# Norms between the stages of a two-block network: order of issue, two engines for the squares, one step less in the mean square

## The chip, the core and the metric

One core of a Trainium2 chip. The metric is device time in microseconds, from the runs of the whole program. The core has TensorE (PE, matmuls and transposes; PEld is its weight load), VectorE (DVE), ScalarE (ACT) and GpSimd (POOL), each with a queue of its own that it works off in order; DMAs are issued from SyncE's queue (SP) and a few from POOL's.

## What is computed

Two blocks on 512 tokens of width 1024, in fp32: a first block with two layers (a token mixer of mLSTM, Fourier and convolution branches, then an MLP with squared ReLU), where layer 0 also works on 256 context tokens, and a second block with two layers of retention, sparse attention and gated linear attention. Around each mixer and MLP stands the same frame:

```python
def rmsnorm(x, g):
    y = xf * lax.rsqrt(jnp.mean(xf * xf, axis=-1, keepdims=True) + EPS)
    return (y * g).astype(x.dtype)

hx = modulate(rmsnorm(x, g_pre_mix[l]), mx[0], mx[1])      # pre-norm, gain and shift
...
x = x + mx[2] * rmsnorm(out_x, g_post_mix[l])              # post-norm and update
hx = modulate(rmsnorm(x, g_pre_mlp[l]), mx[3], mx[4])      # pre-norm of the next stage
x = x + mx[5] * rmsnorm(sq_relu_mlp(hx, w_mlp1[l], w_mlp2[l]), g_post_mlp[l])
```

The post-norm and update of one stage and the pre-norm of the next follow each other directly. This is the work between the stages.

## The kernel before

Tokens are worked on in tiles of 128 rows (four of x, two of the context), and a tile of 128x1024 is kept as two halves of 512 columns. Every fp32 matmul is made of three (mm3, L316 to L318), from a high and a low part of each operand. The weights come by DMA in chunks of 128x1024 (tile `st`), ACT casts the chunk to its high part (`whi`, L283) and DVE subtracts to get the low part (`wlo`, L284). There are three buffers for `st` and four each for `whi` and `wlo` (wload).

The stage ends are project (an output projection, L588 and square_sum) and the last block of mlp (L667, L670). For each token tile i they leave two halves of output times the post gain, and the sum of squares. Then `leave` puts a function `norm` on the list `normed`. When it is called, it does this for the tile:

- update (L503): inv_rms turns the two sums into 1/rms by three POOL steps (L453 add, L454 scale and add EPS, L346 power of -0.5). DVE then makes x = x + o * r for each half, and x goes to DRAM.
- for tile 0, the gains of the next stage (gain_of, L1169), and the steps of the modulation (ada_task, whose products are L381 on POOL with a sum on ACT, and L384 on DVE) that are still missing for them.
- prenorm_a: two squares with row sums on ACT (L465), inv_rms, then the scaling of one half on ACT (L467) and the other on DVE (L468).

It then puts prenorm_b on the list `turned`: per half, four transposes on PE into a PSUM tile `s` (L351; three buffers), gain and shift by turns on ACT (L482) and DVE (L485), and the split into the high part (ACT L312) and the low part (DVE L312) that the next stage's matmuls read.

`flush(n, m)` works off both lists down to n and m entries. `leave` calls it with 1 and 1, so a tile's norm is traced one tile later and its turn two tiles later; `ready`, called at each matmul group of the next stage, works off what that group needs. In flush, `issue_after` queues the ACT instructions of a norm behind the latest square_sum and the PE instructions of a turn behind the latest matmul.

What sets the order: a planner lays out every engine's queue before the run. Of the instructions that it takes to be ready it places the one traced earliest; those traced in a `high_priority` block come before all others, and among themselves in the order of tracing. The weight chunks (DMA, cast, subtraction), project's square_sum and post gain, and the evacuations of PSUM are traced so. The norms and turns of flush are not, except the context's at the very start.

Stretches named A to E in this text are the five stage ends that feed a next stage: A the projection of layer 0 (context and x), B the MLP of layer 0 (both), C the projection and D the MLP of layer 1 (x), E the first projection of the second block. The last projection writes the result.

Of the kernel before, what the change touches and what calls it, by code (L numbers as in the profile page):

```python
# [13 lines left out]
AF = mybir.ActivationFunctionType  # L14
OP = mybir.AluOpType

P = 128
D = 1024
# [3 lines left out]
EPS = 1e-6  # L22
# [203 lines left out]
class Net:  # L226
# [140 lines left out]
    def ada_task(self, w, j, vecs, mods, bias, post=None, key=None):  # L367


        nc = self.nc  # L370
        part = self.small("adp", [P, 2, 8, 2])
        for f in range(8):
            st = self.hp.tile([P, D], F32, tag="sa", name=self.nm("sa"), bufs=NSA)
            nc.sync.dma_start(st, w[f])
            for m, v in enumerate(vecs):
                row = self.cond_row(v)
                for h in range(2):
                    e = slice(512 * h, 512 * h + 512)
                    x, o = self.slot(), part[:, m, f, h:h + 1]
                    if m:  # L380
                        nc.gpsimd.tensor_mul(x, st[:, e], row[:, e])  # L381
                        nc.scalar.activation(x, x, AF.Copy, accum_out=o)
                    else:
                        nc.vector.tensor_tensor_reduce(x, st[:, e], row[:, e], 1.0, 0.0, op0=OP.mult, op1=OP.add,  # L384
                                                       accum_out=o)
            yield
        for m, mod in enumerate(mods):
            e = slice(8 * j, 8 * j + 8)
            nc.vector.tensor_add(mod[:, e], part[:, m, :, 0], part[:, m, :, 1])
            nc.vector.tensor_add(mod[:, e], mod[:, e], bias[:, e])  # L390
            if post is not None:
                g = self.small("gv", [P, 8])
                nc.vector.tensor_mul(g, mod[:, e], post)
                ps = self.psum("s")
                self.transpose(ps[:8, :P], g)
                row = self.small("gvt", [8, P])
                nc.vector.tensor_copy(row, ps[:8, :P])
                d = self.grows[key + (m,)] = self.dp.tile([8, P], F32, tag="gr%d%d%d%d" % (*key, m), name=self.nm("gr"))
                nc.sync.dma_start(d, row)
# [50 lines left out]
    def inv_rms(self, ss):  # L450

        v = self.small("ms", [P, 1])
        self.nc.gpsimd.tensor_add(v, ss[:, 0:1], ss[:, 1:2])  # L453
        self.nc.gpsimd.tensor_scalar(v, v, 1.0 / D, EPS, op0=OP.mult, op1=OP.add)  # L454
        return self.rsqrt(v, 1)

    def square_sum(self, src, acc):
# [2 lines left out]
    def prenorm_a(self, xh):  # L460
        nc = self.nc
        xn = [self.slot(), self.slot()]
        ss = self.small("ss", [P, 2])
        for j in range(2):
            nc.scalar.activation(xn[j], xh[j], AF.Square, accum_out=ss[:, j:j + 1])  # L465
        r = self.inv_rms(ss)
        nc.scalar.activation(xn[0], xh[0], AF.Copy, scale=r)  # L467
        nc.vector.tensor_scalar_mul(xn[1], xh[1], r)  # L468
        return xn
# [78 lines left out]
    def flush(self, n, m):  # L548

        while len(self.normed) > n:  # L550
            with self.tc.issue_after(self.last_sq):
                self.normed.pop(0)[2]()
        while len(self.turned) > m:
            with self.tc.issue_after(self.last_mm):
                self.turned.pop(0)[2]()

    def ready(self, h, i, ahead):
# [609 lines left out]
    def gain_of(self, tag, mod, j, base):  # L1167
        g = self.small(tag, [P, 8])
        self.nc.vector.scalar_tensor_tensor(g, mod[:, 8 * j:8 * j + 8], 1.0, base, op0=OP.add, op1=OP.mult)  # L1169
        return g  # L1170

    def first_block(self):
# [717 lines left out]
```

## Time and profile before

| | before |
|---|---|
| median of 3 runs | 2880.83 us (2879.89 to 2881.83) |
| the profiled execution | 2877.77 us, span of its instructions 2875.7 us |
| mean granted TensorE clock | 0.973 |
| PE busy | 2686.8 us, 93% |
| DVE, ACT, POOL busy | 60%, 40%, 16% |
| DMA | 312.85 MB, 109 GB/s |

The span runs from the first to the last instruction; times in the rows are counted from its start. An engine's busy share is over the whole span, in which stages with different limits follow each other.

### The profile page before, as it was taken

What the parts mean: (1) busy time and instruction counts of PE and PEld (TensorE: products, weight loads), DVE (VectorE), ACT (ScalarE), POOL (GpSimd) and SP (SyncE); (2) the same over time, 40 slices, a digit from 0 to 9 for tenths busy, and PEclk for the clock granted to TensorE, in tenths of its full rate; (3) what the DMA queues carried; (4) which work ended last, traced back from release to release, by engine and by line L of the source; (5) the groups of instructions that cost most, each with busy time, mean ns of one, the idle gap of its engine ahead of it and who ended that gap; (6) DMA issues with size and microseconds to landing.
All of it is one profiled execution on the core that took longest, in us unless ns stands there. A gap on an engine that the chain in (4) does not pass through costs nothing. (4 is left out here: it accounts for less than half of the span.)

```text
span 2875.7 us, 36809 instructions
## 1 busy us (share of the span) xinstructions
PE 2686.8 (93%) x13684; PEld 2161.2 (75%) x13684; DVE 1737.3 (60%) x3619; ACT 1158.1 (40%) x2224; POOL 455.0 (16%) x548
## 2 busy tenths in 40 slices
PE   6877998999999998998999989999999999999998
PEld 2766787888888876787878867776788777767887
DVE  3799756466555578955566457666433567664334
ACT  2644545444222264545323353435222543353222
POOL 2365302233000013201000010010012100101011
PEclk9989999999999999999999999999999999999999
DMA  8322224334433443224464332211132412111223
GB/s 272 115 78 83 90 70 147 125 119 131 139 119 132 131 141 111 88 88 147 159 200 157 115 121 87 83 60 52 37 103 95 147 67 96 52 59 37 96 88 117
DMA packets 101283, 312.85 MB, mean 109 GB/s; under 512 B 11504, under 2 KB 15368, under 8 KB 101104
## 3 DMA queue, kind: packets, MB, share of 16 engines
q1 hardware_dynamic: 100544, 309.64, 32.5%
q8 instruction: 107, 1.75, 0.3%
q0 software_dynamic: 560, 0.86, 0.1%
q14 instruction: 72, 0.59, 0.1%
HBM read 293.43 MB, written 17.03 MB: 108 GB/s over the span
## 5 line engine op out<-in xcount | busy, mean ns | idle before, releaser
L316 PE MATMUL mm<-xhi,whi 128*128 128x512 f32 (+2 forms) x1520 | 598.3, 394 | 41.9 <-DVE sl L779 29.1
L284 DVE TENSOR_TENSOR wlo<-st,whi 128x1024 fp32r<-128x1024 f32 x352 | 448.7, 1280 | 281.9 <-ACT whi L283 276.1
L283 ACT CAST whi<-st 128x1024 fp32r<-128x1024 f32 x352 | 369.9, 1052 | 565.8 <-PE mm L317 284.7
L317 PE MATMUL mm<-xlo,whi 128*128 128x512 f32 (+2 forms) x1520 | 593.3, 390 | 0.4 <-DVE xlo L312 0.2
L318 PE MATMUL mm<-xhi,wlo 128*128 128x512 f32 (+2 forms) x1520 | 592.6, 390 | 0.0
L316 PEld LDWEIGHTS mm<-xhi,whi 128*128 128x128 f32 (+1 forms) x1520 | 291.0, 192 | 101.3 <-issue 22.2
L318 PEld LDWEIGHTS mm<-xhi,wlo 128*128 128x128 f32 (+1 forms) x1520 | 291.1, 192 | 57.8 <-issue 0.3
L317 PEld LDWEIGHTS mm<-xlo,whi 128*128 128x128 f32 (+1 forms) x1520 | 291.3, 192 | 57.4 <-issue 1.5
L316 PE MATMUL mm<-whi,sl 128*128 128x512 f32 x640 | 249.5, 390 | 2.5 <-DVE spare L667 1.6
L317 PE MATMUL mm<-wlo,sl 128*128 128x512 f32 x640 | 249.8, 390 | 0.7 <-DVE wlo L284 0.6
L318 PE MATMUL mm<-whi,sl 128*128 128x512 f32 x640 | 249.2, 389 | 0.0
L316 PE MATMUL mm<-whi,xhi 128*128 128x512 f32 x576 | 230.3, 401 | 3.3 <-ACT xhi L312 3.3
L317 PE MATMUL mm<-wlo,xhi 128*128 128x512 f32 x576 | 230.0, 399 | 0.2
L318 PE MATMUL mm<-whi,xlo 128*128 128x512 f32 x576 | 228.5, 397 | 0.4 <-DVE xlo L312 0.2
L384 DVE CUSTOM_DVE_ANT_0 sl<-sa,crow 128x512 f32<-128x512 f32 x256 | 190.2, 774 | 31.3 <-DMA sa<-in_ada 15.9
L351 PE MATMUL s<-ident,sl 128*128 128x128 f32 (+2 forms) x756 | 125.0, 286 | 79.5 <-ACT sl L467 16.3
L351 PEld LDWEIGHTS s<-ident,sl 128*128 128x128 f32 (+2 forms) x756 | 88.7, 144 | 132.6 <-issue 42.8
L381 POOL TENSOR_TENSOR sl<-sa,crow 128x512 f32<-128x512 f32 x96 | 149.7, 1584 | 162.0 <-DMA sa<-in_w_ada 117.1
L316 PEld LDWEIGHTS mm<-whi,sl 128*128 128x128 f32 x640 | 120.1, 188 | 28.6 <-DVE spare L667 2.4
L317 PEld LDWEIGHTS mm<-wlo,sl 128*128 128x128 f32 x640 | 120.1, 188 | 27.6 <-DVE wlo L284 3.0
L318 PEld LDWEIGHTS mm<-whi,sl 128*128 128x128 f32 x640 | 120.2, 188 | 24.8
L453 POOL TENSOR_TENSOR ms<-psum_sq 128x1 f32<-128x1 f32 x28 | 6.3, 227 | 805.5 <-ACT sl L458 805.5
(373 smaller groups left out, 4549.7 us busy)
## 6 DMA issues: line engine op xcount, KB each, us to landing
st<-in_w_mlp SPq DMA_DIRECT2D x128, 512.0 KB, 4.4
st<-in_win_a SPq DMA_DIRECT2D x116, 512.0 KB, 3.2
sa<-in_w_ada SPq DMA_DIRECT2D x80, 512.0 KB, 3.4
sa<-in_ada SPq DMA_DIRECT2D x48, 512.0 KB, 3.5
st<-in_win_b SPq DMA_DIRECT2D x40, 512.0 KB, 3.7
st<-in_w_out SPq DMA_DIRECT2D x32, 512.0 KB, 3.2
xres<-sl SPq DMA_DIRECT2D x48, 256.0 KB, 4.9
sl<-xres SPq DMA_DIRECT2D x48, 256.0 KB, 5.3
```

The source lines that it names most:

```text
L283: nc.scalar.copy(hi, st)
L284: nc.vector.tensor_sub(lo, st, hi.bitcast(F32))
L316: mm(ps, l[0], r[0], start=first, stop=False)
L317: mm(ps, l[0], r[1], start=False, stop=False)
L318: self.last_mm = mm(ps, l[1], r[0], start=False, stop=last).ins
L351: self.nc.tensor.transpose(out, src, self.ident[:p, :p])
L381: nc.gpsimd.tensor_mul(x, st[:, e], row[:, e])
L384: nc.vector.tensor_tensor_reduce(x, st[:, e], row[:, e], 1.0, 0.0, op0=OP.mult, op1=OP.add, accum_out=o)
L453: self.nc.gpsimd.tensor_add(v, ss[:, 0:1], ss[:, 1:2])
```

## The change

Four edits:

- flush: the norms and the turns are traced in a `high_priority` block, as the weights are.
- prenorm_a: the square and row sum of half 0 goes to DVE as one multiply with an accumulator; that of half 1 stays on ACT.
- inv_rms: POOL adds the two sums and D * EPS in one instruction, so the root is 1/32 of what it was (D = 1024).
- the factor 32 that is then missing goes into the gains: one more DVE instruction of 128x8 in gain_of, and a changed instruction for the post gains in ada_task.

```diff
             if post is not None:
                 g = self.small("gv", [P, 8])
-                nc.vector.tensor_mul(g, mod[:, e], post)
+                nc.vector.scalar_tensor_tensor(g, mod[:, e], 32.0, post, op0=OP.mult, op1=OP.mult)
...
     def inv_rms(self, ss):
         v = self.small("ms", [P, 1])
-        self.nc.gpsimd.tensor_add(v, ss[:, 0:1], ss[:, 1:2])
-        self.nc.gpsimd.tensor_scalar(v, v, 1.0 / D, EPS, op0=OP.mult, op1=OP.add)
+        self.nc.gpsimd.tensor_scalar(v, ss[:, 0:1], ss[:, 1:2], D * EPS, op0=OP.add, op1=OP.add)
         return self.rsqrt(v, 1)
...
         ss = self.small("ss", [P, 2])
-        for j in range(2):
-            nc.scalar.activation(xn[j], xh[j], AF.Square, accum_out=ss[:, j:j + 1])
+        nc.vector.tensor_tensor_reduce(xn[0], xh[0], xh[0], 1.0, 0.0, op0=OP.mult, op1=OP.add, accum_out=ss[:, 0:1])
+        nc.scalar.activation(xn[1], xh[1], AF.Square, accum_out=ss[:, 1:2])
...
     def flush(self, n, m):
         while len(self.normed) > n:
-            with self.tc.issue_after(self.last_sq):
+            with self.tc.issue_after(self.last_sq), self.tc.high_priority():
                 self.normed.pop(0)[2]()
         while len(self.turned) > m:
-            with self.tc.issue_after(self.last_mm):
+            with self.tc.issue_after(self.last_mm), self.tc.high_priority():
                 self.turned.pop(0)[2]()
...
     def gain_of(self, tag, mod, j, base):
         g = self.small(tag, [P, 8])
         self.nc.vector.scalar_tensor_tensor(g, mod[:, 8 * j:8 * j + 8], 1.0, base, op0=OP.add, op1=OP.mult)
+        self.nc.vector.tensor_scalar_mul(g, g, 32.0)
         return g
```

## Rows read from the trace of the kernel before

**Rows 1.** The page: busy time of engines, and TensorE's in 40 slices (tenths).
```profile
PE 2686.8 (93%) x13684; PEld 2161.2 (75%) x13684; DVE 1737.3 (60%) x3619; ACT 1158.1 (40%) x2224; POOL 455.0 (16%) x548
...
PE   6877998999999998998999989999999999999998
```

**Rows 2.** Windows A to E: length; busy PE, PEld, DVE, ACT, POOL; granted clock; DMA.
```profile
447.00:514.00 67.00, 56.76 (x332) 50.23 (x331) 47.82 (x90) 41.55 (x102) 25.96 (x46) 0.92 0.33 116
1004.00:1056.00 52.00, 44.83 (x210) 34.81 (x209) 38.25 (x70) 32.37 (x75) 10.97 (x34) 1.00 0.44 149
1304.00:1346.00 42.00, 31.16 (x176) 26.62 (x175) 25.13 (x44) 25.06 (x56) 9.10 (x26) 0.88 0.39 125
1675.00:1714.00 39.00, 33.21 (x149) 26.14 (x148) 26.76 (x47) 24.11 (x54) 7.88 (x24) 0.91 0.45 153
2267.00:2312.00 45.00, 39.09 (x177) 30.81 (x176) 27.28 (x52) 27.96 (x65) 10.23 (x30) 0.92 0.39 127
```

**Rows 3.** Waits of PE in the whole span: total us, times, longest us.
```profile
PE s L351 <- ACT sl L467: 16.3, 9, 4.9
PE s L351 <- ACT sl L482: 14.4, 6, 4.6
...
PE mm L316 <- ACT xhi L312: 7.5, 6, 2.1
...
PE mm L317 <- DVE wlo L284: 2.7, 4, 1.4
```

**Rows 4.** Timeline of ACT in E: start, us, instruction, count [idle before <-releaser].
```profile
2277.61 1.05 ACT L283 CAST whi<-st 128x1024 fp32r<-128x1024 f32 x1
...
2280.56 1.04 ACT L283 CAST whi<-st 128x1024 fp32r<-128x1024 f32 x1
...
2282.28 0.80 ACT L482 ACTIVATE sl<-s,mod,G 128x128 f32<-128x128 f32 x2
...
2284.86 0.46 ACT L482 ACTIVATE sl<-s,mod,G 128x128 f32<-128x128 f32 x1 [1.17 <-DVE sl L485]
```

**Rows 5.** Timeline of DVE in E.
```profile
2276.92 0.72 DVE L485 TENSOR_SCALAR sl<-s,G,mod 128x128 f32<-128x128 f32 x2
...
2280.42 3.49 DVE L284 TENSOR_TENSOR wlo<-st,whi 128x1024 fp32r<-128x1024 f32 x3
...
2285.06 0.75 DVE L503 SCALAR_TENSOR_TENSOR sl<-sl,rq_y,sl 128x512 f32<-128x512 f32 x1
...
2288.35 0.68 DVE L312 TENSOR_TENSOR xlo<-sl,xhi 128x512 fp32r<-128x512 f32 x1
```

**Rows 6.** Timeline of PE in E.
```profile
2285.37 0.66 PE L351 MATMUL s<-ident,sl 128*128 128x128 f32 x4 [3.27 <-ACT sl L482]
2286.82 0.80 PE L316 MATMUL mm<-whi,xhi 128*128 128x512 f32 x1 [0.80 <-ACT xhi L312]
```

**Rows 7.** Single lines in the whole span: count, shortest/median/longest ns, first and last start.
```profile
L465 ACT ACTIVATE sl<-sl x60: 612/630/648, 6.8 to 2293.7; 128x512 f32<-128x512 f32 x60
...
L384 DVE CUSTOM_DVE_ANT_0 sl<-sa,crow x256: 618/687/1783, 92.5 to 1570.8; 128x512 f32<-128x512 f32 x128
...
L454 POOL TENSOR_SCALAR ms<-ms x58: 187/190/693, 13.1 to 2870.1; 128x1 f32<-128x1 f32 x58
...
L381 POOL TENSOR_TENSOR sl<-sa,crow x96: 1261/1462/4032, 96.9 to 689.8; 128x512 f32<-128x512 f32 x96
...
L503 DVE SCALAR_TENSOR_TENSOR sl<-sl,rq_y,sl x52: 740/747/1773, 449.1 to 2871.7; 128x512 f32<-128x512 f32 x52
```

**Rows 8.** Timeline of ACT in A, around the context's first norm.
```profile
461.29 0.63 ACT L382 ACTIVATE sl<-sl 128x512 f32<-128x512 f32 x1 [4.47 <-POOL sl L381]
...
463.60 0.61 ACT L465 ACTIVATE sl<-sl 128x512 f32<-128x512 f32 x1
```

**Rows 9.** Timeline of POOL at the kernel's end.
```profile
2869.85 0.19 POOL L453 TENSOR_TENSOR ms<-psum_sq 128x1 f32<-128x1 f32 x1 [4.11 <-ACT sl L458]
2870.13 0.19 POOL L454 TENSOR_SCALAR ms<-ms 128x1 f32<-128x1 f32 x1
```

## Prediction

> **What bounds the kernel now.** I read the page's busy times first: TensorE is busy for 93% of the span, in nearly every slice, and VectorE for 60% [rows 1]. So the time is TensorE's work plus the stretches in which it waits or runs at half clock, and the change can only move those. The slices are too coarse to show where they are, so I went to the stretches between stages, one after each post-norm that feeds a next stage: A after the first output projection, B after the first MLP, C after the second projection, D after the second MLP, E after the first of the two projections of the second block. The windows view has a row for each [rows 2]. Stretch less busy PE gives idle of 10.24, 7.17, 10.84, 5.79 and 5.91 us, 40.0 us in all. The granted clock in them is 0.92, 1.00, 0.88, 0.91 and 0.92; TensorE has only the levels 2.4 and 1.2 GHz here, and a time at half clock loses half of itself, so one minus this share times the stretch is what the clock costs: 5.4, 0, 5.0, 3.5 and 3.6 us, 17.5 in all. **57.5 us** (2.0%) is thus all that the norms between stages can give back, and 15.6, 7.2, 15.8, 9.3 and 9.5 us are the shares of A to E. The list of what PE waited for says the same from the other side [rows 3]: transposes waiting for the normalised tile (ACT L467, 16.3 us) or for a PSUM buffer that the affine step still reads (ACT L482, 14.4), and matmuls waiting for the split operand (ACT L312, 7.5), 38.2 us together, a few of them at the kernel's start. The weights' low parts cost 2.7 us in the whole run: the weights come early, the norms late.
>
> **Why they are late** is to be seen in E, engine by engine. On ACT three casts of next-stage weights run at 2277.61 to 2281.60, and the affine steps of a tile that PE had already turned wait behind them until 2282.28 and 2284.86 [rows 4]. On DVE the affine halves of 2276.92 are followed by one update half and then by 3.49 us of weight subtractions, so the second update half comes at 2285.06 [rows 5]. PE stands for 3.27 us for that L482, and its first matmul of the next stage is at 2286.82 [rows 6]; the half clock of rows 2 follows on such stands. C and D have the same form.
>
> **The change part by part.** (1) *Raised priority* in flush: updates, squares, reciprocal roots, scalings, transposes, affines and splits of a pending tile now stand before every weight chunk that is traced later; the weights were raised already. It removes nothing and issues nothing new; it swaps the order. On POOL the roots come ahead of background products; on SP the block holds only the modulation loads still missing in A, which now go ahead of the next stage's weight loads, and the result's stores at the very end (the other loads and stores of x are traced outside it). A raised update or scaling that waits for its root holds up what stands behind it on DVE or ACT: weight halves, and through them PE. In E the two L482 halves need not wait for the casts: they could stand where the first cast stands, at 2277.61, 4.7 and 7.3 us sooner. PE's 3.27 us go. What is next late is the weights: the last of four halves lands at 2283.91 (2280.42 plus 3.49). Behind the norms it moves by what is pending there [rows 5]: at least the second update half, two affines and the new square (0.75 + 0.72 + 0.69 = 2.2 us), at most all that DVE does now from 2283.91 to 2289.03 less one weight half of 1.16, and the square (5.12 - 1.16 + 0.69 = 4.7): 2286.1 to 2288.6. PE, which stops at 2282.10 and has four more transposes (0.66) and a hand-over, would begin the next stage at about 2282.9 [rows 6] and want the last half 18 matmuls later, at 0.22 us each (39.09 us for the 177 of E [rows 2]) at 2286.9. So it waits 0 to 1.7 us there, and E gains 3.9 us of start less that, plus part of the 3.6 us of clock: 4 to 6, I take 5, 53% of its 9.5. The same share of C and D (25.1 us) is 13.3. Sum for C to E **18.3**.
>
> (2) *Squares on two engines.* Now ACT does both, 0.63 us each [rows 7]. After it ACT does one while DVE does the other; DVE's multiply with an accumulator stands in the modulation's products, L384, at 0.62 to 1.78, median 0.69 [rows 7]. I take the median; about one square, 0.6 us, is saved per tile, and nothing (or 1.2 us lost) when DVE is full or blocked. ACT loses 30 x 0.6 us, DVE gains 30 x 0.7; in the five stretches DVE is busy for 60 to 74% [rows 2], so it is hidden where there is slack and costs up to 0.69 per tile where DVE sets the pace, which I expect in B alone (two streams, six tiles, short matmuls). In A there is a second gain: the second square sat on ACT until 463.60, because ACT had been given a modulation product's sum first and idled 4.47 us for POOL [rows 8]. With one square on ACT, in the place where the first stood, ahead of those sums, PE's wait for that tile's L467 can go (at most 4.9 us, the longest [rows 3]). It may also stay, since the modulation's rest is traced inside the raised block, ahead of the squares. I take **6** of A's 15.6 and **2** of B's 7.2.
>
> (3) *One step less in the mean square.* Each POOL step takes 0.28 us from start to start [rows 9]; it falls out of all 58 roots. Of these two per tile lie in the chains above, inside the bounds already counted. One is bare: the last tile of the kernel, **0.3**. The step that is left reads a per-row scalar on POOL, which no row shows; the nearest rows are the old step's 0.187 to 0.693 [rows 7], and I take 0.19, as both plain [128,1] steps cost that. At 0.69 it would be a loss of 0.2 at the end and 0.4 in each chain.
>
> (4) *The factor 32* is nine more DVE instructions on 128x8 (nine calls of gain_of), each below the 0.36 us of an affine step on 128x128 [rows 5], so under 3.3 us of DVE in all, and a changed multiplier in the gate vectors. The modulation's work comes ahead of its use everywhere but in A, where two of the nine stand before the first affine: hidden, or 0.7 us there.
>
> One row speaks against part 2. L503, a DVE update with two SBUF inputs, takes 0.74 us and 1.77 at worst, L384 0.69 and 1.78; POOL's products, L381, take 1.46 [rows 7]. If the long ones are those beside POOL's products, a square in A can cost 1.1 us more on DVE than on ACT, whose squares never take over 0.65. The Trainium skill (SBUF — State Buffer, "Who interferes with whom") has a rule for it: a DVE instruction with two SBUF inputs contends with a GpSimd instruction that reads SBUF, and ScalarE waits on no other engine. By that rule the edit puts a step that nothing could disturb on an engine that POOL can block; the spread of the rows agrees.
>
> **Sum:** 18.3 + 6 + 2 + 0.3 = 26.6, less 3.6 for DVE's added load in B (six squares of 0.69, 4.1 us, half of it bare) and for squares behind POOL in A (three of the six, 1.1 each and half of it bare, 1.6): 23 us. The profiled execution took 2877.77 us (span 2875.7 and 2.1 around it), so 2854.8 for one like it; the median of the runs is 3.06 us above it, which gives **2857.8**.
>
> **The rivals.** *Chain only.* The planner orders what is ready; if its own estimate of the chains makes the norms ready only when the casts are already placed, the priority changes little, and what is left is the shorter chain: 0.6 + 2 x 0.28 = 1.2 us, once per boundary, 6, and 0.3 at the end: 2874.5. For: a cast is 1.05 us on ACT and its subtraction 1.16 on DVE [rows 4, 5], and neither is interrupted once begun. Against: in E the L482 halves were ready from 2277 and stood through three casts.
>
> *Weights late (slower).* In C, D and E the last three weight halves go behind all pending norm work, on DVE which is busy for 60 to 69% there. It decides when the last half lands more than 2.9 us behind its present 2283.91, that is past 2286.82, where PE starts now: at the upper bound (4.7 us) PE starts no sooner and waits 1.8 us more. If one more tile's norm joins the queue (two updates of 0.74 and a square of 0.69, 2.2 us [rows 7]), it waits 4.0: 3 x 4 = 12 us, less some 3 that the shorter chain still gives: 2890. For: only four buffers of each weight part, so halves cannot come earlier than the last tile's matmuls free them. Against: the halves wanted first are loaded long before.
>
> *Squares blocked.* In A all six squares run beside POOL's products at 1.78 us, 6.6 us more on DVE, and in B all six are bare: A and B give nothing, and what is left is 18.6 less 3.6, 15: 2866. The rule above is this rival's; it lies on the same side as the forecast.
>
> *More than that.* The planner lays out every queue anew, and TensorE also waits in the mixers; those waits can shift either way by some 5 us without a mechanism that I could name. With three quarters of the bound recovered the time would be 2838.
>
> **How the numbers follow.** Forecast (a gain of 14 to 35 us) 0.60; squares blocked 0.12; more than that 0.05; chain only 0.11; weights late 0.12. The range takes the low end of the last gain and reaches past no change to the near side of the weights' rival: 2838 to 2883. A measurement of this kernel can tell about 0.2%, 5.8 us, from no change: the chain rival, 6.3 us, sits on that edge, so I split it, and give faster 0.77, same 0.11, slower 0.12.
>
> **What would show it.** Right: in E and C the affines L482 before the casts L283 and the update halves L503 back to back, PE's waits for L467 and L482 under 15 us together (30.7 now), granted clock near 1.0 in C to E, L454 with 58 instructions and L453 gone, L465 with 30. Wrong: PE waits for L284 or L283 in C to E above 5 us, DVE squares of 1.7 us in A, or idle PE in the five stretches still near 40 us. If these come down as said and the total does not, the time was lost again in the mixers.

## The result and the profile after

The changed kernel takes 2902.89 us (median of 4 runs, 2894.61 to 2905.14) against 2880.36 for the one before on the same chip: ratio 1.0068, 95% interval 1.0048 to 1.0088. It is slower by 0.7%, 19.6 us by the ratio, where 23 us less were forecast. The profiled execution, the shortest of the four, took 2894.61 us; its span is 2892.7 (17.0 more), mean granted clock 0.971. In the changed kernel a line between 455 and 1168 has a number smaller by one: the affine on ACT is L481 (was L482), on DVE L484 (L485), the scaled copies L466 and L467 (L467, L468), the update L502 (L503), the square on DVE L463, on ACT L464.

The page of the kernel after, as in [rows 1]:

```profile
PE 2689.7 (93%) x13684; PEld 2163.3 (75%) x13684; DVE 1758.5 (61%) x3688; ACT 1141.6 (39%) x2164; POOL 440.3 (15%) x490
...
PE   6877897999999988998999999999999999999998
```

DVE has 21.2 us more and ACT 16.5 less, roughly the 30 moved squares. PE is as busy as before (2.9 us more). The windows of the five stretches A to E, set so that each holds about the matmuls of [rows 2] (columns as there):

```profile
449.50:524.30 74.80, 57.61 (x333) 49.97 (x332) 53.30 (x104) 39.13 (x90) 24.97 (x34) 0.91 0.30 103
1013.00:1067.50 54.50, 46.48 (x211) 36.57 (x210) 43.22 (x84) 30.40 (x67) 10.07 (x23) 0.97 0.40 137
1314.80:1358.90 44.10, 30.86 (x178) 26.46 (x177) 27.97 (x52) 22.85 (x48) 7.70 (x18) 0.88 0.36 118
1692.30:1732.60 40.30, 33.27 (x149) 25.95 (x148) 29.50 (x56) 22.16 (x47) 7.26 (x16) 0.92 0.42 145
2281.70:2330.30 48.60, 41.04 (x179) 31.40 (x178) 30.15 (x64) 25.31 (x57) 9.10 (x24) 0.93 0.37 122
```

The lengths add up to 262.3 us against 245.0 in [rows 2]: 17.3 us more, as much as the span grew. A has 7.8 of it, E 3.6, B 2.5, C 2.1, D 1.3. So the loss sits in the stretches that were to give. Outside them gains and losses cancel: by the edges of the same rows 2.5 us are lost ahead of A and 4.4 between C and D, and 3.9 are won between D and E. Idle PE in the five stretches is 53.0 us (40.0 before), and what the half clock costs there, one minus the granted clock times the length, is 20.3 us (17.5).

What PE waited for in the whole span (total us, times, longest us), as in [rows 3]:

```profile
PE s L351 <- ACT sl L481: 24.2, 10, 7.6
...
PE s L351 <- ACT sl L466: 10.3, 6, 4.9
PE mm L316 <- ACT xhi L312: 8.8, 7, 2.1
...
PE mm L317 <- DVE clo L312: 4.9, 2, 3.6
PE s L351 <- DVE sl L467: 4.9, 6, 2.4
...
PE mm L317 <- DVE wlo L284: 3.0, 5, 1.4
```

The scaled copy on ACT costs PE 6.0 us less than before, the affine 9.8 us more, and waits for DVE have grown: for the context's split `clo` (5.6 us over two lines, 1.8 before) and for the scaled copy of the other half (none before). The weights' low parts (L284) cost what they did: they are not what became late.

Why the affine is late is to be read in E. Timelines of the kernel after, first ACT, then DVE, then PE (start, us, instruction, count, idle before and what ended it):

```profile
2301.47 0.45 ACT L481 ACTIVATE sl<-s,mod,G 128x128 f32<-128x128 f32 x1
2301.81 0.63 ACT L464 ACTIVATE sl<-sl 128x512 f32<-128x512 f32 x1
...
2304.76 0.72 ACT L466 ACTIVATE sl<-sl,rq_y 128x512 f32<-128x512 f32 x1 [2.23 <-POOL rq_y L346]
2305.39 0.44 ACT L481 ACTIVATE sl<-s,mod,G 128x128 f32<-128x128 f32 x1
2307.05 0.46 ACT L481 ACTIVATE sl<-s,mod,G 128x128 f32<-128x128 f32 x1 [1.22 <-DVE sl L484]
```

```profile
2302.76 0.68 DVE L463 CUSTOM_DVE_ANT_0 sl<-sl 128x512 f32<-128x512 f32 x1
...
2305.27 1.42 DVE L502 SCALAR_TENSOR_TENSOR sl<-sl,rq_y,sl 128x512 f32<-128x512 f32 x2 [1.50 <-POOL rq_y L346]
2306.61 0.41 DVE L484 TENSOR_SCALAR sl<-s,G,mod 128x128 f32<-128x128 f32 x1
```

```profile
2307.56 1.11 PE L351 MATMUL s<-ident,sl 128*128 128x128 f32 x4 [3.09 <-ACT sl L481]
```

On ACT the square (L464) and the scaled copy (L466) of a later tile stand between two affines, and ACT idles 2.23 us for POOL's root. On DVE the square, 1.50 us of waiting and both update halves stand ahead of the affine L484 of 2306.61. ACT's affine of 2307.05 waits for that one, and PE, which waits 3.09 us, for ACT's: the four affines of a half go by turns through DVE and ACT, so what stands ahead of one of them on either queue holds all that follow. Before, weights' casts and subtractions stood in that place [rows 4, 5]. From 2302.3 to 2307.5 neither queue has one any more, and the norms have taken their place.

### The profile page after: what moved, and what is told of

Its sections match the earlier page's. It is cut to its first block, busy times and chain, and to the rows that moved or that the text cites. A ratio compares the mean times of both kernels' runs of the same rounds, so it can differ in the third digit from the quotient of the medians.

```text
span 2892.7 us, 36720 instructions
## 1 busy us (share of the span) xinstructions
PE 2689.7 (93%) x13684; PEld 2163.3 (75%) x13684; DVE 1758.5 (61%) x3688; ACT 1141.6 (39%) x2164; POOL 440.3 (15%) x490
## 5 line engine op out<-in xcount | busy, mean ns | idle before, releaser
L284 DVE TENSOR_TENSOR wlo<-st,whi 128x1024 fp32r<-128x1024 f32 x352 | 448.7, 1280 | 280.6 <-ACT whi L283 275.0
L317 PE MATMUL mm<-xlo,whi 128*128 128x512 f32 (+2 forms) x1520 | 593.8, 391 | 0.2
L317 PEld LDWEIGHTS mm<-xlo,whi 128*128 128x128 f32 (+1 forms) x1520 | 291.6, 192 | 57.0 <-issue 1.5
L317 PE MATMUL mm<-wlo,sl 128*128 128x512 f32 x640 | 250.6, 392 | 1.6 <-DVE wlo L284 1.6
L317 PE MATMUL mm<-wlo,xhi 128*128 128x512 f32 x576 | 229.9, 399 | 0.2
L351 PE MATMUL s<-ident,sl 128*128 128x128 f32 (+2 forms) x756 | 125.5, 286 | 87.2 <-ACT sl L481 24.2
L381 POOL TENSOR_TENSOR sl<-sa,crow 128x512 f32<-128x512 f32 x96 | 144.2, 1526 | 163.0 <-DMA sa<-in_w_ada 94.2
L317 PEld LDWEIGHTS mm<-wlo,sl 128*128 128x128 f32 x640 | 120.6, 188 | 28.5 <-DVE wlo L284 3.7
L316 PEld LDWEIGHTS mm<-whi,xhi 128*128 128x128 f32 x576 | 109.7, 190 | 31.2 <-ACT xhi L312 6.8
```

Of the source, the lines that this page charges most:

```text
L284: nc.vector.tensor_sub(lo, st, hi.bitcast(F32))
L316: mm(ps, l[0], r[0], start=first, stop=False)
L317: mm(ps, l[0], r[1], start=False, stop=False)
L351: self.nc.tensor.transpose(out, src, self.ident[:p, :p])
```

## The experiments

Times are given as (ratio - 1) times 2882 us. All kernels are the one before with the edit named, or the changed one with an edit taken back.

**The parts one by one.** The edits are the diff's own: the two `high_priority()` in flush alone (prio), the square on DVE alone (squares), the shorter mean square with its factor 32 alone (step), and the changed kernel without the two `high_priority()` (no_prio).

> The kernel before with the raised priority alone (updates, norms and turns). Theory Q (queue order: the raised norm of a later tile, whose scaled copy waits for POOL's mean square, is put ahead of the affines and the splits of a tile that PE is waiting for; and the first halves of several turns are taken ahead of the second half of one): slower by 10 to 20 us, PE's waits for the affines and scaled copies together no smaller than the 30.7 us of before. Theory S (the moved square is the whole loss): 0 to 23 us faster, with those waits below 20 us.

> The kernel before with the first half's square on DVE alone. Theory S (the moved square lengthens DVE's queue, on which an affine, a subtraction of the weights' split or the other scaled copy then comes late): slower by 8 to 20 us, with new waits of PE for DVE of 5 us or more. Theory Q: within 5 us of before, and waits of PE for DVE under 3 us.

> The kernel before with the shorter mean square alone (POOL's two steps in one, the factor 32 in the gains and gate rows). Both theories: 0 to 2 us faster. If the factor's instructions on DVE in the layer-0 projection weigh more than the prediction said: 3 to 8 us slower, with its gap in that stage.

> The changed kernel without the raised priority (squares on two engines and the shorter mean square stay). Theory Q: within 5 us of before. Theory S: slower than before by 8 to 20 us, as the whole change. If the loss needs both (raised norms and a longer DVE queue): near before here, and near before with the priority alone too.

Measured: prio 1.0048 (1.0031 to 1.0066), +13.8 us; squares 1.0010 (0.9998 to 1.0022), +2.9; step 0.9986 (0.9977 to 0.9995), -4.0; no_prio 0.9991 (0.9980 to 1.0003), -2.6. The raised priority alone makes 13.8 of the 19.6 us, and without it no loss is left (no_prio). The moved square alone is about nothing, the shorter mean square a small gain, nominally larger than the 0 to 2 us that were expected. Theory S falls.

**Norms or turns.** The raised block around the norms alone or the turns alone, and inside prenorm_b around its two halves (flush sets `raised` around the turn):

```diff
-            with self.tc.issue_after(self.last_sq):                            # prio_norm
+            with self.tc.issue_after(self.last_sq), self.tc.high_priority():
...
-            with self.tc.issue_after(self.last_mm):                            # prio_turn
+            with self.tc.issue_after(self.last_mm), self.tc.high_priority():
...
+            with self.tc.high_priority() if self.raised else ExitStack():      # prio_pe
                 for f in range(4):
                     self.transpose(ps[:, P * f:P * f + P], xn[j][:, P * f:P * f + P])
...
+            with self.tc.high_priority() if self.raised else ExitStack():      # prio_aff
                 (the four affines and the split)
```

> The kernel before with the turns alone raised (transposes, affines, split). Theory T (the raised transposes stand in PE's queue ahead of products whose operands are ready, and PE then waits for the scaled copies and the affines): slower by 8 to 16 us, like the raised priority as a whole (14 us). Theory N (the raised norms stand ahead of affines and splits on ACT and DVE): within 5 us of before, or faster.

> The kernel before with the updates and norms alone raised. Theory N: slower by 8 to 16 us. Theory T: within 5 us of before, or up to 5 us faster. If the loss needs both at one level, neither half shows more than 5 us.

> The kernel before with the transposes of the turns alone raised (affines and split at their old priority). Theory T: slower by 5 to 16 us, since the place in PE's queue is the cause. Theory N: within 5 us of before.

> The kernel before with the affines and the split of the turns alone raised (transposes at their old priority). This is what the prediction's second step described: affines ahead of the weights' casts. Theory T: 0 to 8 us faster than before, with PE's waits for the affines under 10 us. Theory N: within 5 us of before. If the affines are held by something else than their place (the norm's chain through POOL, the psum buffers), the same time as before.

Measured: prio_turn 0.9996 (0.9987 to 1.0005), -1.2 us; prio_norm 1.0056 (1.0043 to 1.0068), +16.1; prio_pe 1.0006 (0.9997 to 1.0015), +1.7; prio_aff 0.9976 (0.9967 to 0.9985), -6.9. My first reading, that raised transposes block PE's queue (theory T), falls at once: it is the norms (theory N). The 6.9 us of prio_aff are a little more than N expected and lie in T's range, but T's own two kernels, prio_turn and prio_pe, show no loss. Stretch B of prio_norm shows how the norms cost. The timelines of DVE, ACT and PE:

```profile
1035.53 1.42 DVE L503 SCALAR_TENSOR_TENSOR sl<-sl,rq_y,sl 128x512 f32<-128x512 f32 x2 [1.90 <-POOL rq_y L346]
1036.86 0.68 DVE L667 TENSOR_TENSOR sl<-sl,mm 128x512 f32<-128x512 f32 x1
1037.46 2.36 DVE L284 TENSOR_TENSOR wlo<-st,whi 128x1024 fp32r<-128x1024 f32 x2
1039.73 0.48 DVE L468 TENSOR_SCALAR sl<-sl,rq_y 128x512 f32<-128x512 f32 x1
1040.12 1.05 DVE L485 TENSOR_SCALAR sl<-s,G,mod1c 128x128 f32<-128x128 f32 x3
```

```profile
1040.57 0.81 ACT L482 ACTIVATE sl<-s,mod1c,G 128x128 f32<-128x128 f32 x2 [2.94 <-DVE sl L485]
```

```profile
1033.68 0.39 PE L318 MATMUL mm<-whi,sl 128*128 128x512 f32 x1
1041.08 1.97 PE L351 MATMUL s<-ident,sl 128*128 128x128 f32 x8 [7.01 <-ACT sl L482]
```

DVE's affine L485 comes at 1040.12, behind a wait for POOL, a raised update, an evacuation (L667), two weight subtractions and a scaled copy. ACT's L482 waits for it, and PE for that: 7.01 us. In the whole span PE's wait for L482 is 31.6 us here, 14.4 in [rows 3]; with the affines raised instead (prio_aff) the same line is

```profile
PE s L351 <- ACT sl L467: 20.2, 10, 4.8
...
PE s L351 <- ACT sl L485: 1.7, 3, 1.3
```

(its L485 is the affine on ACT). So the affines' place was worth moving, and moving the norms with them undid it.

**Place or wait.** Two parts of the norm were raised singly, and POOL's chain was taken out of the norms, once with them at the old priority and once raised:

```diff
+                with self.tc.high_priority():                   # prio_upd
                     self.update(o, sums, xh, q["st"], i)
...
+                with self.tc.high_priority():                   # prio_na
                     xn = self.prenorm_a(xh)
...
     def inv_rms(self, ss):                                      # nomean, nomean_norm
+        if self.in_norm:
+            return self.rconst
```

> The kernel before with the updates alone raised (POOL's mean square of the product and L503); squares and scaled copies of the norms keep their old priority. Theory U (the raised update stands on DVE ahead of affines and weights' splits and holds them while POOL forms its factor, as in the stretch 1033 to 1041 us of the kernel with raised norms): slower by 10 to 18 us, like the raised norms (16 us). Theory C (it is the scaled copies on ACT that hold the affines behind them): within 5 us of before.

> The kernel before with the second half of the norms alone raised (squares, POOL's mean square, scaled copies); the update keeps its old priority. If each instruction raised ahead of the affines costs its share: the rest of the raised norms' 16 us beside the 9 us of the update, 4 to 9 us slower. If only the update matters: within 3 us of before.

> The kernel before with a constant in place of the reciprocal root mean square in the updates and norms between the stages, so POOL's chain is left out there. It is the base for the next kernel: 5 to 40 us faster than before by both theories, since the chain of 2 to 3 us stands in front of each last tile.

> The same with the updates and norms raised; it leaves out the same part. If the raised norms cost time because they hold a queue while POOL's chain runs (theory W, the wait at the head of DVE's and ACT's queues), this is within 5 us of the kernel with the constant and the old priority. If they cost it by their own work, which comes ahead of affines and splits (theory P, the place), the loss of some 16 us stays.

Measured: prio_upd 1.0029 (1.0018 to 1.0040), +8.4 us; prio_na 0.9999 (0.9990 to 1.0008), -0.3; nomean 0.9909 (0.9894 to 0.9923), -26.2; nomean_norm 0.9964 (0.9950 to 0.9978), -10.4. Raising the norms costs 15.8 us even where no norm waits for POOL (give or take some 6 by the two intervals), as much as with POOL's chain (16.1). So theory W falls for norms that are raised alone, and P stands: the wait for the root in the timelines above is what one sees, but not what it costs; if the root were there at once, the raised work itself would stand in the place. PE's wait for the affine grows without the chain too, from 14.5 us in nomean to 26.0 in nomean_norm. B of nomean_norm, ACT and then PE (here L469 is the square, L471 the scaled copy, L486 the affine):

```profile
1029.55 1.03 ACT L283 CAST whi<-st 128x1024 fp32r<-128x1024 f32 x1
1030.49 0.63 ACT L469 ACTIVATE sl<-sl 128x512 f32<-128x512 f32 x1
...
1031.11 0.71 ACT L471 ACTIVATE sl<-sl,rconst 128x512 f32<-128x512 f32 x1
1031.72 0.79 ACT L486 ACTIVATE sl<-s,mod1c,G 128x128 f32<-128x128 f32 x2
```

```profile
1032.22 1.11 PE L351 MATMUL s<-ident,sl 128*128 128x128 f32 x4 [4.33 <-ACT sl L486]
```

Of the two parts of the norm only the update costs when raised alone, 8.4 us, less than theory U expected and more than C. The squares and scaled copies raised alone cost nothing. What ACT's affine (L482) waited for in the whole span tells the two apart (us, times), prio_upd first, then prio_na:

```profile
  DVE sl L485: 45.9, 22
```

```profile
  DVE sl L485: 37.5, 18
```

Before it is 39.8 us, 20 times. The update is DVE's work: raised, it stands ahead of DVE's affine, and ACT's affine waits for that. Raised squares and copies lengthen PE's wait for the affines as well (20.4 us for 14.4), but shorten that for the copies by about as much (9.9 for 16.3). The two parts add up to half of the 16 us. What the rest needs of both at once is open.

**Why the parts don't add.** The changed kernel with both squares on ACT (no_squares), with the norms at the old priority (after_turn), with only affines and split raised (after_aff), and the one before with raised priority and the moved square (prio_sq):

```diff
-        nc.vector.tensor_tensor_reduce(xn[0], xh[0], xh[0], ...)                   # no_squares
-        nc.scalar.activation(xn[1], xh[1], AF.Square, accum_out=ss[:, 1:2])
+        for j in range(2):
+            nc.scalar.activation(xn[j], xh[j], AF.Square, accum_out=ss[:, j:j + 1])
...
-            with self.tc.issue_after(self.last_sq), self.tc.high_priority():       # after_turn
+            with self.tc.issue_after(self.last_sq):
```

> The changed kernel with both squares on ACT again (raised priority and the shorter mean square stay). If the single effects add (14 less 4): 10 us slower than before. If the moved square costs more under raised norms (theory M: on DVE it stands ahead of affines and weights' splits): 8 to 13 us slower, and so 7 to 12 us faster than the whole change. If the raised priority and the shorter mean square together make the rest: 17 to 20 us slower, as the whole change.

> The changed kernel with the updates and norms back at their old priority (turns raised, square moved, mean square shorter). By theory P (raised updates and norms come ahead of affines with their own work) the whole loss goes: 0 to 5 us faster than before. If the moved square costs by itself 6 us or more, it is 2 to 6 us slower than before.

> The changed kernel with only the affines and split of the turns raised, the square on DVE. Against the same with both squares on ACT (13 us faster than before): by theory M about the same, 10 to 14 us faster than before, as nothing of the norm is raised. If the moved square costs by itself: 5 to 10 us faster.

> The kernel before with the raised priority and the moved square, the mean square as before. By theory M (on DVE, ahead of affines and splits, the square costs under raised norms): 18 to 30 us slower than before, more than the raised priority alone (14 us). If the shorter mean square is what goes badly with the moved square: 10 to 16 us slower, less than the whole change (20 us).

Measured: no_squares 0.9983 (0.9973 to 0.9992), -4.9 us; after_turn 0.9966 (0.9953 to 0.9979), -9.8; after_aff 0.9965 (0.9953 to 0.9977), -10.1; prio_sq 1.0074 (1.0062 to 1.0087), +21.3. One line taken back, the norms' priority, turns the change from 19.6 us slower to 9.8 faster. Under raised norms the moved square costs 7.5 us with the old mean square and 24.5 with the short one, while alone it cost 2.9: the extra cost is what theory M says, and prio_sq and after_aff came out in its range. That after_turn would be 9.8 us faster is more than theory P's 0 to 5, and that the changed kernel without the moved square would be faster than before (no_squares) no theory had. Nor do the waits of prio_sq follow M alone: PE waits only 6.1 us for the affines there, but 28.7 for the split on ACT (`xhi`, 7.5 before), 8.6, 7.1 and 5.7 of it at once in C, D and E. DVE is the queue of half the affines and of every low part. In A one line shows it, the subtraction that makes the last low part of the context tiles: the second of a pair that runs from 500.94 to 502.22 in the kernel after, while in no_squares it is at 488.75. DVE's timeline after, then that of no_squares:

```profile
497.10 1.42 DVE L502 SCALAR_TENSOR_TENSOR sl<-sl,rq_y,sl 128x512 f32<-128x512 f32 x2
...
500.94 1.28 DVE L312 TENSOR_TENSOR clo<-sl,chi 128x512 fp32r<-128x512 f32 x2
```

```profile
488.75 0.68 DVE L312 TENSOR_TENSOR clo<-sl,chi 128x512 fp32r<-128x512 f32 x1
489.35 0.68 DVE L587 TENSOR_TENSOR sl<-mm,sl 128x512 f32<-128x512 f32 x1
...
490.93 1.42 DVE L502 SCALAR_TENSOR_TENSOR sl<-sl,rq_y,sl 128x512 f32<-128x512 f32 x2 [0.90 <-POOL rq_y L346]
```

In no_squares the context is finished first and x's updates come behind it; after, two update pairs of x and two moved squares, at 489.29 and 494.18, come first. PE's wait for `clo` at L317 is 4.9 us after and 2.2 in no_squares. But that the short mean square turns prio's +13.8 into -4.9 I cannot explain by its own length. In A of prio the last `clo` is at 497.92, in no_squares at 488.75: the planner laid the queues another way. Why these few tenths tip it is not shown by any run.

**A version that beats both.** The two edits that gained singly, put together: only the affines and split raised, and the shorter mean square (aff_step); beside it the whole turn raised with the same mean square (turn_step).

```diff
             with self.tc.issue_after(self.last_mm):                               # aff_step
+                self.raised = True
                 self.turned.pop(0)[2]()
+                self.raised = False
...
+            with self.tc.high_priority() if self.raised else ExitStack():
                 (the four affines and the split)
...
-            with self.tc.issue_after(self.last_mm):                               # turn_step
+            with self.tc.issue_after(self.last_mm), self.tc.high_priority():
```

> The kernel before with the affines and split of the turns raised and the shorter mean square: updates and norms at their old priority, both squares on ACT. If the two gains measured singly (0.24% and 0.14%) add up: 8 to 14 us faster than before. If the one takes the place of the other: 4 to 8 us faster.

> The kernel before with the turns raised as a whole (transposes too) and the shorter mean square; updates and norms at their old priority, both squares on ACT. If the raised transposes take nothing back: 11 to 16 us faster than before, like affines and split alone with the shorter mean square (13 us). If they do: 3 to 9 us faster.

Measured: aff_step 2869.32 us, ratio 0.9948 (0.9931 to 0.9964), -15.0 us; turn_step 0.9995 (0.9984 to 1.0006), -1.4. The first is a little better than the best of its expectations, the second worse than both. So the transposes take most of it back when they are raised too, as they did with the old mean square (prio_turn -1.2, prio_aff -6.9); with the square on DVE they do not (after_turn and after_aff are equal), and alone they cost 1.7 us (prio_pe). Why is open.

turn_step also limits what was said of the norms. no_squares is turn_step with the norms raised too, and it is not slower (-4.9 against -1.4 us). So raised norms cost 15 to 16 us beside the old mean square (prio_norm; prio against prio_turn), 29 in the changed kernel (against after_turn), and nothing beside the short mean square with both squares on ACT. The moved square turns its sign as well: with the turns raised and the short mean square it gains 8.4 us (after_turn against turn_step), with only affines and split raised it loses 4.9 (after_aff against aff_step). Every edit makes the planner lay out all queues anew, and how far that alone moves the time no run shows. Windows of aff_step for A to E:

```profile
448.00:511.40 63.40, 54.31 (x333) 47.88 (x331) 47.90 (x91) 41.56 (x102) 25.36 (x34) 0.97 0.37 124
1001.70:1051.30 49.60, 45.45 (x211) 36.77 (x211) 38.32 (x70) 31.93 (x75) 10.29 (x23) 0.97 0.46 157
1300.00:1340.30 40.30, 31.67 (x176) 27.15 (x175) 25.16 (x44) 25.21 (x56) 7.84 (x18) 0.87 0.41 134
1671.80:1708.10 36.30, 33.08 (x150) 25.88 (x149) 26.23 (x47) 23.90 (x54) 7.00 (x16) 0.95 0.49 160
2261.20:2302.50 41.30, 36.67 (x177) 29.26 (x176) 27.02 (x53) 27.87 (x65) 8.46 (x22) 1.00 0.43 139
```

They add up to 230.9 us, 14.1 less than in [rows 2]: idle 29.7 us (40.0), cost of the half clock 10.4 (17.5). The span of this execution is 9.2 us shorter, so 4.9 us were lost outside the stretches; 1.8 of them go with the runs of the kernel before beside it, which are that much slower than in the table of times before (2882.61 us for 2880.83).

**All in one view.** PE's waits in the whole span, summed for the scaled copies (two lines), the affines and the splits of the norms, against the time; the last column, which is not in the sum, is ACT's wait for DVE's affine:

| kernel | copies | affines | splits | sum, us | time, us | ACT for DVE's affine |
|---|---|---|---|---|---|---|
| before | 16.3 | 14.4 | 10.8 | 41.5 | 0 | 39.8 |
| after | 15.2 | 24.2 | 16.2 | 55.6 | +19.6 | 47.0 |
| prio | 13.0 | 20.7 | 14.5 | 48.2 | +13.8 | 44.4 |
| prio_norm | 12.8 | 31.6 | 7.5 | 51.9 | +16.1 | 47.7 |
| prio_upd | 13.3 | 20.8 | 10.1 | 44.2 | +8.4 | 45.9 |
| prio_na | 9.9 | 20.4 | 14.0 | 44.3 | -0.3 | 37.5 |
| prio_sq | 18.3 | 6.1 | 36.0 | 60.4 | +21.3 | 45.1 |
| prio_turn | 23.8 | 8.9 | 10.1 | 42.8 | -1.2 | 36.1 |
| turn_step | 19.0 | 7.3 | 10.9 | 37.2 | -1.4 | 39.0 |
| no_squares | 10.3 | 19.8 | 9.0 | 39.1 | -4.9 | 42.3 |
| prio_aff | 20.2 | 1.7 | 13.6 | 35.5 | -6.9 | 33.3 |
| after_turn | 19.5 | 4.4 | 12.4 | 36.3 | -9.8 | 34.5 |
| aff_step | 18.1 | 1.5 | 11.9 | 31.5 | -15.0 | 34.4 |

Over all 18 kernels that have the norms' whole arithmetic (before and after among them) time goes with the sum by 1.33 us per us, correlation 0.96. In the last column the five kernels that are 8 us slower or more have 44.4 to 47.7 us, the other thirteen 33.3 to 42.3. The stretches say the same as the times: A to E together are 15.9 us longer than before in prio, 15.8 in prio_norm, 20.5 in prio_sq and 1.5, 8.3 and 14.1 shorter in no_squares, prio_aff and aff_step, each within 3.5 us of the time's change. With both squares on ACT, raised norms shorten the wait for the copies by 3 to 6 us and lengthen that for the affines by 5 to 17; raised affines and splits do the reverse, at a profit (prio_aff, aff_step).

## Why the prediction was wrong

- **Bound: held.** A to E were the place: they lengthen by 17.3 us, the span by 17.0, and in aff_step they give 14.1 of the 57.5 us that they hold.
- **Step 1, raised priority, 18.3 us: this is the step that failed.** Its one worked example put the affines ahead of the weights' casts, and asked which weight half comes late next. That part exists, in a smaller size: prio_aff does just this, it is 6.9 us faster in all, and C, D and E are 0.5, 1.9 and 2.6 us shorter in it, 5.0 in place of 18.3. The example also moved the affine of 2284.86 by ACT's order alone, 7.3 us, where [rows 4] mark it as released by DVE's L485: DVE's queue sets it as much as ACT's. But the edit raises updates, squares and scaled copies as well. The prediction counted them only as load in front of the weights ("the second update half, two affines and the new square"), as if the affines came first among them; it never asked what they do to the affines of an earlier tile. The code has the answer ready: flush traces a tile's norm ahead of the turn of the tile before it, and among raised instructions the earlier traced goes first. Raised alone, a tile's updates and norms cost 16.1 us (prio_norm), on top of raised turns 15.0 (prio against prio_turn), and the prediction's sentence on a raised update holding up what stands behind it named the weights as victim, not the affines. Why the same raising costs nothing in no_squares stays open.
- **Step 2, squares, 6 us in A and 2 in B: wrong.** PE's wait for that tile's scaled copy is 4.87 us, 4.57 before, and the moved square alone made the kernel 2.9 us slower (interval from 0.6 faster to 6.3 slower) where 8 less 3.6 were to be gained. The ACT square that remains did not take the place ahead of the modulation's sums but went behind them, and the DVE square beside POOL's products took 1.74 us. ACT, DVE and POOL in A, after:

```profile
463.84 0.63 ACT L382 ACTIVATE sl<-sl 128x512 f32<-128x512 f32 x1 [5.27 <-POOL sl L381]
...
466.14 0.61 ACT L464 ACTIVATE sl<-sl 128x512 f32<-128x512 f32 x1
```

```profile
462.59 1.77 DVE L384 CUSTOM_DVE_ANT_0 sl<-sa,crow 128x512 f32<-128x512 f32 x1
...
464.29 1.74 DVE L463 CUSTOM_DVE_ANT_0 sl<-sl 128x512 f32<-128x512 f32 x1
```

```profile
462.11 3.38 POOL L381 TENSOR_TENSOR sl<-sa,crow 128x512 f32<-128x512 f32 x2 [4.29 <-DMA sa<-in_w_ada]
```

  Of the six squares in A this one alone is long (the median of the six is 0.684) and it alone ran beside an L381, so the rival with all six blocked did not come. The Trainium skill (SBUF — State Buffer, "Who interferes with whom") has DVE instructions with two SBUF inputs contend with GpSimd instructions that read SBUF; the trace agrees, since the two DVE rows shown, which begin while L381 runs, take 1.77 and 1.74 and the median of all squares is 0.684.
- **Step 3, the mean square: right in sign, mis-sized.** The one step takes 0.30 us, the two took 0.19 each, and the root starts 0.39 behind it:

```profile
2887.09 0.30 POOL L453 TENSOR_SCALAR ms<-psum_sq 128x1 f32<-128x1 f32 x1 [4.27 <-ACT sl L457]
2887.48 0.56 POOL L346 TENSOR_TENSOR rq_y<-ms,mhalf 128x1 f32<-128x1 f32 x1
```

  Two pitches of 0.28 became one of 0.39, so 0.17 per chain in place of 0.28. Alone it gave 4.0 us in all (interval 1.4 to 6.6), against the 0.3 that the sum had outside its bounds. Two roots at each of five boundaries and one at the end would give 1.9 us at 0.17, an estimate; what makes the rest, if it is real, is not shown.
- **Step 4, the factor 32: right.** Nine instructions of 0.17 us; the two in A stand on DVE ahead of an idle of 0.89 us.
- **The rivals.** "Weights late" had the sign and its mechanism did not happen: PE's waits for L284 are 3.0 us against 2.7. "Chain only" and "squares blocked" missed the sign. The rival that came true, norms ahead of affines, was not on the list, so a chance of 0.12 for slower was too low. Of the signs named, PE's waits for the scaled copy on ACT and the affine were to fall from 30.7 below 15 us; they rose to 34.5. Of the signs of being wrong two came: a DVE square of 1.74 us in A, and idle PE in the five stretches, which did not fall from 40.0 us but rose to 53.0.

## What to carry to other kernels

Of a chain of steps that ends at the engine that sets the pace, try to raise the last step, the one that frees its buffer or makes its operand, before the whole chain: here the upper steps of a later tile went ahead of the last step of an earlier one, also where they had nothing to wait for. Where the last step goes by turns through two engines, look at both queues. When an edit raises a block, list every instruction in it and ask of each which other raised one it can now overtake. Effects of order don't add: take each part alone and each part away, before one is called harmless.

## What the runs showed of the hardware

In the engines' own durations two things stand out: the DVE square of 1.74 us next to POOL's product (0.684 otherwise), and the single POOL step with two per-row scalars, 0.30 us where the plain step takes 0.19. Unexpected was the slope: a microsecond of PE's waits for the norms went with 1.33 us of time. The granted clock is part of it: between after and aff_step, A's clock is 0.91 and 0.97 and E's 0.93 and 1.00, and what the half clock costs in the five stretches is 20.3 and 10.4 us. That the clock makes all of the third beyond one for one is not shown.
